# The expert layer's first part: GpSimd's arithmetic moved to VectorE, and one-hots of eight tokens made at once

## The chip, the cores and the metric

One NeuronCore of a Trainium2 chip runs the whole program; the other seven cores are idle. The metric is device time in microseconds (us) of one execution. The kernel before takes 5999.07 us (median of three executions, 5996.86 to 6004.16).

## What is computed

A two-layer backbone of a latent generator: 512 latent and 256 context tokens of width 1024. Layer 0 mixes tokens with an mLSTM, layer 1 with a Mamba-2 scan, and each is followed by a channel mixer out of 16384 single-neuron experts ("PEER"), which is where this change lies:

```python
def block(xb):                                   # 128 tokens
    q = (xb @ wq).reshape(P_BLOCK, P_HEADS, 2, P_DK // 2)
    s = jnp.einsum('thcd,hcnd->thcn', q, sub_keys)
    s_top, i_top = lax.top_k(s, P_TOPK)          # 16 of 128 keys, both halves
    ...
    best_s, best_j = lax.top_k(cand_s, P_TOPK)   # 16 of 256 pairs
    idx = jnp.take_along_axis(cand_i, best_j, axis=-1)
    gate = jax.nn.softmax(best_s, axis=-1)
    act = jax.nn.gelu(jnp.einsum('td,thkd->thk', xb, u[idx]))
    return jnp.einsum('thk,thkd->td', gate * act, v[idx])
```

Each token thus picks 8 heads x 16 experts, an expert being a row of `u` and a row of `v`, and adds up gate x gelu(u.x) x v.

## The kernel before

**Two ways for the experts.** Of the four latent tiles of 128 tokens, three are done densely by `peer_lat` (L895): the scores of *all* 16384 experts are computed, multiplied by a table of gates that is zero where an expert wasn't picked, and multiplied with `v`. The fourth tile, and the context tokens before it, gather their rows with indirect DMAs (`gather_steps`, issued by GpSimd at L864, read by VectorE at L871 and L882).

**The expert layer's first part**, once in each layer, is the stage that the change touches. It has two streams of work that are written interleaved:

- *Score steps* (`prefix`, L907, which calls `scores`, L973). A step covers 128 experts. It loads 512 KB of `u` (`raw`), and `wpair` (L170) splits each half into a rounded part `whi` (ScalarE, L177) and the rest `wlo` (L179, a subtraction of 128x512 elements); 24 products on TensorE (L212 to L214, 128x384) and a gelu (L981) follow, and the result goes to the DRAM tensor `aD`. There are NPRE = 66 such steps. `wlo` is made by VectorE, but for the first UPX = 36 steps by GpSimd: 36 x 2 = 72 subtractions in each layer.
- *Gate steps* (`gate_steps`, L983), which write the gate table `gD`. For each of three tiles `select` (L803) first picks the 16 best of each head on VectorE (L793 to L845, three large operations a head at L832 to L834). Then, four tokens at a time, VectorE compares the expert's two indices with 0..127 (`oh`, L1016, both at once, 128x1024 elements in bfloat16), GpSimd multiplies the first one-hot by a power of two from the gate (`oa`, L1019, 128x512), VectorE the second by the mantissa (`og`, L1021, 128x1024), and 8 products of 128x128 on TensorE (L1026) make the gates of these four tokens, which ScalarE copies out (`sg`, L1028). 32 groups a tile, 96 in a layer, 192 in all.

```python
due = (i2 + 1) * PER          # PER = 2.2
while made < due:
    made += 1
    next(gates_, None)
```

So about two gate steps are written behind each score step, and some gather steps of the fourth tile beside them (`tick`, at rates R_PRA, R_PRE and R_PR1). This is the written order only: a scheduler takes all instructions and puts them in an order of its own on each engine, by its model of when their inputs are ready. An engine then keeps to that order. The dense part behind the stage (`dense`, L1033) needs the gates of all tokens, so it starts when the last gate group is written.

Buffers that matter: `oh` 2, `oa` 2, `og` 2, `sg` 2, the halves `whi` and `wlo` 3 each, two banks `mx` for the gate products.

Of the kernel before, what the change touches and what calls it, by code (L numbers as in the profile page):

```python
# [8 lines left out]
F32 = mybir.dt.float32  # L9
# [36 lines left out]
DTN, SB0, ZD, HV = 1, 0, 1, 1  # L46
PER = 2.2
NPG1, R_PR1 = 46, 1.0
GOP = 1
UP = "v"  # L50
UPX = 36
GS = 10
CSP = 3
SEL = 99
# [15 lines left out]
def backbone(ctx: ExitStack, tc: tile.TileContext, A: dict, out: bass.AP):  # L70
# [732 lines left out]
    def select(pp, vt, it, tag=""):  # L803

        itf = pp.tile([P, PH, 2, TOPK], F32, tag="itf", name="itf", bufs=1)
        nc.vector.tensor_copy(itf.rearrange("p h c k -> p (h c) k"), it)
        nc.vector.tensor_scalar(itf[:, :, 0], itf[:, :, 0], float(PK), None, op0=OP.mult)
        v4 = vt.rearrange("p (h c) k -> p h c k", c=2)
        csb, cib = big_g(pp), big_g(pp)
        cs, ci = [b[:, :PH * NCAND].rearrange("p (h c) -> p h c", h=PH) for b in (csb, cib)]  # L810
        for dst_, a in ((cs, v4), (ci, itf)):
            o = 0
            for r, n in SEGS:
                (nc.gpsimd if CSP & (1 if dst_ is cs else 2) else nc.vector).tensor_tensor(dst_[:, :, o:o + n], a[:, :, 0, r:r + 1].to_broadcast([P, PH, n]),
                                        a[:, :, 1, 0:n], OP.add)
# [12 lines left out]

        pick = csb[:, :NCAND * TOPK].rearrange("p (c k) -> p c k", k=TOPK)
        oh = cib[:, 512:1024].bitcast(BF16)[:, :NCAND * TOPK].rearrange("p (c k) -> p c k", k=TOPK)  # L830
        for hd in range(PH):
            nc.vector.tensor_tensor(oh, placek, bjb[:, hd, None, :].to_broadcast([P, NCAND, TOPK]), OP.is_equal)  # L832
            nc.vector.tensor_tensor(pick, oh, ci[:, hd, :, None].to_broadcast([P, NCAND, TOPK]), OP.mult)  # L833
            nc.vector.tensor_reduce(fi[:, hd], pick.rearrange("p c k -> p k c"), AX.X, OP.add)  # L834
            if hd % SEL == SEL - 1:
                yield
        idx = pp.tile([P, PH * TOPK], I32, tag="idx" + tag, name="idx", bufs=2)
        nc.vector.tensor_copy(idx, fi.rearrange("p h k -> p (h k)"))
        gt = pp.tile([P, PH, TOPK], F32, tag="gt" + tag, name="gt", bufs=2)
# [55 lines left out]
    def peer_lat(i, h, pp, then=lambda: None, close=lambda: None):  # L895


        nt = LAT // P
        nd = NDENSE
        TD = nd * P  # L900
        gD = tc.dram_tile([PK // GJ, P, TD, GJ], F32, name=f"gD{i}")
        aD = tc.dram_tile([NPRE, P, TD], F32, name=f"aD{i}")
        with tc.tile_pool(name="pt", bufs=1, reuse_waits="tile") as xp:
            xh = xp.tile([P, 8, LAT], F32R, name="pinh")
            xl = xp.tile([P, 8, LAT], F32R, name="pinl")

            def prefix(i2):  # L907
                w = xp.tile([P, TD], F32, tag="w", name="w", bufs=3)
                scores(xp, i, i2, xh, xl, TD, w, nc.gpsimd if i2 < UPX or UP[i2 % len(UP)] == "p" else None)
                nc.sync.dma_start(aD[i2], w)  # L910

            back["rate"] = R_WQ
            vt, it = peer_scores(xp, i, 0, LAT, h, xh, xl)
            back["rate"] = 0.0
            before, aside = back["steps"], []

            def rest():
                yield from before
                aside.append(then())
                yield  # L920
                for t in range(nd, nt):
                    yield from gather_steps(pp, i, 0, h(t), h(t), vt[t], it[t])

            back["steps"] = rest()
            with tc.tile_pool(name="pb", bufs=1, reuse_waits="tile") as bp:
                iot4 = bp.tile([P, P, 4], BF16, name="iot4")
                nc.vector.tensor_copy(iot4, iotk[:, :, None].to_broadcast([P, P, 4]))
                gates_ = itertools.chain(*[gate_steps(pp, bp, vt[t], it[t], gD, t, iot4) for t in range(nd)])
                made = 0
                for i2 in range(NPRE):  # L930
                    prefix(i2)
                    due = (i2 + 1) * PER
# [3 lines that stand above are left out]
                    tick((R_PRE if i2 >= NPG else R_PRA) if i == 0 else (R_PR1 if i2 >= NPG1 else 0))  # L936
                for _ in gates_:
                    pass
            with tc.tile_pool(name="pd", bufs=1, reuse_waits="tile") as dp:
                acc = dense(xp, dp, i, gD, aD, nd, xh, xl)  # L940
        close()
        return aside[0], peer_out(i, h, acc, nd)
# [27 lines left out]
                nc.vector.tensor_tensor(y, y, g, OP.mult)  # L970
                nc.vector.tensor_tensor(h(t), y, b, OP.add)

    def scores(xp, i, i2, xh, xl, TD, w, eng):  # L973

        so = smb()[:, :TD]
        for half, (uh, ul) in enumerate(wpair(A[f"uT{i}"][i2].rearrange("h p c -> p h c"), eng=eng)):
            for k in range(4):
                s = slice(k * P, (k + 1) * P)
                kk = half * 4 + k
                mm3(so, uh[:, s], ul[:, s], xh[:, kk, :TD], xl[:, kk, :TD], kk == 0, kk == 7)  # L980
        nc.scalar.activation(w, so, AF.Gelu_apprx_tanh)  # L981

    def gate_steps(pp, bp, vt, it, gD, t, iot4):  # L983
# [13 lines left out]
        nc.tensor.transpose(o[:, 2 * P:3 * P], gt, ident)  # L997

        ct = bp.tile([P, 3, P], BF16, tag="ct", name="ct", bufs=2)
        nc.scalar.copy(ct[:, :2].rearrange("p c t -> p (c t)"), o[:, :2 * P])  # L1000
        gs = bp.tile([P, 2, P], F32, tag="gs", name="gs", bufs=1)
        g_, e_ = gs[:, 0], gs[:, 1]
        nc.scalar.copy(g_, o[:, 2 * P:3 * P])
# [6 lines left out]
        nc.vector.scalar_tensor_tensor(cm[:, 1], g_, 2.0 ** GS, cm[:, 0], OP.mult, OP.subtract)  # L1010
        for q in range(P // GT):
            sg = bp.tile([P, PK // GJ, GT, GJ], F32, tag="sg", name="sg", bufs=2)
            for r in range(GT // 4):
                n = slice(q * GT + r * 4, q * GT + r * 4 + 4)
                oh = bp.tile([P, 2, P, 4], BF16, tag="oh", name="oh", bufs=2)
                nc.vector.tensor_tensor(oh, iot4[:, None].to_broadcast([P, 2, P, 4]),  # L1016
                                        ct[:, 0:2, None, n].to_broadcast([P, 2, P, 4]), OP.is_equal)
                oa = bp.tile([P, P, 4], BF16, tag="oa", name="oa", bufs=2)
                (nc.gpsimd if GOP else nc.vector).tensor_tensor(oa, oh[:, 0], ct[:, 2, None, n].to_broadcast([P, P, 4]), OP.mult)  # L1019
                og = bp.tile([P, 2, P, 4], F16, tag="og", name="og", bufs=2)  # L1020
                nc.vector.tensor_tensor(og, oh[:, 1, None].to_broadcast([P, 2, P, 4]),  # L1021
                                        cm[:, :, None, n].to_broadcast([P, 2, P, 4]), OP.mult)
                g4 = mxb()
                for k in range(4):
                    for u in range(2):
                        nc.tensor.matmul(g4[:, k * P:(k + 1) * P], oa[:, :, k], og[:, u, :, k], start=u == 0, stop=u == 1)  # L1026
                yield
                nc.scalar.activation(sg[:, :, r * 4:r * 4 + 4], g4.rearrange("p (t g j) -> p g t j", t=4, j=GJ),  # L1028
                                     AF.Copy, scale=2.0 ** -GS)
            c0 = t * P + q * GT  # L1030
            nc.sync.dma_start(gD[:, :, c0:c0 + GT].rearrange("g p t j -> p g t j"), sg)

    def dense(xp, dp, i, gD, aD, nd, xh, xl):  # L1033
# [4 lines left out]
        def weights(i2):  # L1038
# [554 lines left out]
```

## Time and profile before

| | us |
|---|---|
| median of the three executions | 5999.07 |
| the profiled execution, on the device | 6006.95 |
| its span, first to last instruction | 6004.9 |
| TensorE busy (products) | 5313.7 (88%) |
| VectorE busy | 4773.5 (79%) |
| GpSimd busy | 2319.6 (39%) |
| ScalarE busy | 2265.9 (38%) |

The stage lies at about 2376 to 2941 us (layer 0) and 4640 to 5166 us (layer 1), counted from the first comparison of the key scores (L793) to the last gate group. In the page, PE is TensorE's products, PEld its weight loads, DVE VectorE, ACT ScalarE, POOL GpSimd and SP the queue of plain DMAs. Shares of busy time are averages over stages with different limits, so the stage is looked at by itself. The granted clock of TensorE is 0.935 over the span.

### The profile page before, as it was taken

How to read it: one execution, taken by the hardware profiler on the slowest of the kernel's cores; microseconds unless marked ns; L12 is line 12 of the kernel's file. 1: busy time of each engine (PE TensorE's matmuls, PEld its weight loads, DVE VectorE, ACT ScalarE, POOL GpSimd, SP SyncE). 2: the span in 40 equal slices, each digit the busy share in tenths (PEclk: the TensorE clock that was granted, in tenths of full speed). 3: DMA queues.
4: the chain of work that ended last, by engine and by line, in shares of the span. 5: the costliest groups of instructions: out<-in, count | busy, mean ns of one | idle time of the engine just before them, and what ended most of it. 6: DMA issues, size and time to landing. Idle time of an engine off the chain costs nothing. (4 is left out here: it accounts for less than half of the span.)

```text
span 6004.9 us, 77193 instructions
## 1 busy us (share of the span) xinstructions
PE 5313.7 (88%) x25708; PEld 4364.4 (73%) x25708; DVE 4773.5 (79%) x8768; ACT 2265.9 (38%) x4218; POOL 2319.6 (39%) x1908
## 2 busy tenths in 40 slices
PE   6899899999997876888799999789877989799998
PEld 4678777766663454788678999667656879678997
DVE  6744567777676788999888889777886999788988
ACT  4543454322222332334333333443323334333333
POOL 1300001355544345474333445433441475433443
PEclk8999999999998897989899999899978989899999
DMA  6755454898879987456698999333334347799996
GB/s 210 239 185 157 159 169 157 294 338 302 305 251 325 331 292 244 142 171 214 227 324 320 341 340 330 131 94 108 95 105 127 108 142 243 269 339 325 345 340 235
DMA packets 655801, 1406.98 MB, mean 234 GB/s; under 512 B 62761, under 2 KB 237497, under 8 KB 650921
## 3 DMA queue, kind: packets, MB, share of 16 engines
q1 hardware_dynamic: 507944, 865.11, 43.6%
q0 software_dynamic: 147456, 536.94, 25.4%
q8 instruction: 202, 3.31, 0.2%
q14 instruction: 199, 1.62, 0.1%
HBM read 1278.10 MB, written 123.70 MB: 233 GB/s over the span
## 5 line engine op out<-in xcount | busy, mean ns | idle before, releaser
L177 ACT CAST whi<-raw 128x512 fp32r<-128x512 f32 x2032 | 1227.2, 619 | 1810.1 <-PE mm L213 614.5
L179 DVE TENSOR_TENSOR wlo<-raw,whi 128x512 fp32r<-128x512 f32 x1787 | 1240.4, 710 | 437.7 <-ACT whi L177 419.6
L864 POOL DMA_INDIRECT g<-in_u_dram,idx x512 | 654.6, 1279 | 1055.0 <-PE mx L214 324.2
L864 POOL DMA_INDIRECT g<-in_v_dram,idv x512 | 685.5, 1339 | 686.0 <-DVE acc L882 293.5
L882 DVE SCALAR_TENSOR_TENSOR acc<-g,act,acc 128x1024 f32<-128x1024 f32 x508 | 664.4, 1308 | 149.0 <-DMA g<-in_v_dram,idv 145.8
L871 DVE CUSTOM_DVE_ANT_0 g<-g,xb 128x1024 f32<-128x1024 f32 x512 | 627.6, 1230 | 185.8 <-DMA g<-in_u_dram,idx 181.4
L214 PE MATMUL sm<-pinh,wlo 128*128 128x384 f32 x2048 | 708.5, 347 | 19.2 <-POOL wlo L179 11.7
L212 PE MATMUL sm<-pinh,whi 128*128 128x384 f32 x2048 | 710.4, 347 | 15.8 <-ACT w L981 13.3
L213 PE MATMUL sm<-pinl,whi 128*128 128x384 f32 x2048 | 707.1, 345 | 0.0
L179 POOL TENSOR_TENSOR wlo<-raw,whi 128x512 fp32r<-128x512 f32 x245 | 365.3, 1501 | 430.5 <-ACT whi L177 403.6
L213 PE MATMUL mm<-wlo,wh 128*128 128x512 f32 x1024 | 399.6, 393 | 17.1 <-DVE wlo L179 17.1
L214 PEld LDWEIGHTS sm<-pinh,wlo 128*128 128x128 f32 x2048 | 395.3, 193 | 26.1 <-POOL wlo L179 15.5
L212 PEld LDWEIGHTS sm<-pinh,whi 128*128 128x128 f32 x2048 | 396.2, 193 | 23.8 <-ACT w L981 14.9
L213 PEld LDWEIGHTS sm<-pinl,whi 128*128 128x128 f32 x2048 | 396.1, 193 | 5.5
L214 PE MATMUL mm<-whi,wl 128*128 128x512 f32 x1024 | 394.7, 392 | 1.6 <-DVE wl L190 1.6
L212 PE MATMUL mm<-whi,wh 128*128 128x512 f32 x1024 | 362.2, 395 | 35.3 <-ACT wh L189 33.1
L1019 POOL TENSOR_TENSOR oa<-oh,ct 128x512 bf16<-128x512 bf16 x192 | 283.2, 1488 | 249.0 <-PE mx L1026 117.9
L213 PE MATMUL mm<-xcl,whi 128*128 128x256 f32 (+1 forms) x1024 | 349.7, 346 | 6.6 <-DVE xcl L190 6.6
L212 PE MATMUL mm<-xch,whi 128*128 128x256 f32 (+1 forms) x1024 | 344.8, 349 | 6.3 <-ACT xch L189 4.0
L214 PE MATMUL mm<-xch,wlo 128*128 128x256 f32 (+1 forms) x1024 | 332.4, 350 | 19.4 <-DVE wlo L179 19.1
L212 PE MATMUL mm<-inh,whi 128*128 128x512 f32 (+1 forms) x768 | 283.8, 373 | 10.4 <-ACT cva L405 4.7
L213 PE MATMUL mm<-inl,whi 128*128 128x512 f32 (+1 forms) x768 | 278.4, 364 | 0.0
(478 smaller groups left out, 11493.7 us busy)
## 6 DMA issues: line engine op xcount, KB each, us to landing
raw<-in_uT_dram SPq DMA_DIRECT2D x256, 512.0 KB
raw<-in_v_dram SPq DMA_DIRECT2D x256, 512.0 KB
raw<-in_w_qk_dram SPq DMA_DIRECT2D x128, 512.0 KB
raw<-in_ada_w_dram SPq DMA_DIRECT2D x96, 512.0 KB
raw<-in_w_up_dram SPq DMA_DIRECT2D x96, 512.0 KB
gD<-sg SPq DMA_DIRECT2D x48, 1024.0 KB
gtb<-gD SPq DMA_DIRECT2D x32, 1536.0 KB
raw<-in_s_in_dram SPq DMA_DIRECT2D x72, 512.0 KB
```

The lines of the kernel that those rows point to most:

```text
L177: nc.scalar.copy(hi, raw[:, u])
L179: (eng or next(los["eng"])).tensor_tensor(lo, raw[:, u], hi.bitcast(F32), OP.subtract)
L212: nc.tensor.matmul(o, sh, mh, start=start, stop=False)
L213: nc.tensor.matmul(o, sh, ml, start=False, stop=False)
L214: last["pe"] = nc.tensor.matmul(o, sl, mh, start=False, stop=stop)
L864: d = nc.gpsimd.indirect_dma_start(out=g_, out_offset=None, in_=tab, in_offset=bass.IndirectOffsetOnAxis(ap=ix[:, k:k + 1], axis=0))
L871: nc.vector.tensor_tensor_reduce(out=g_, in0=g_, in1=xb, scale=1.0, scalar=0.0, op0=OP.mult, op1=OP.add, accum_out=act[:, k:k + 1])
L882: nc.vector.scalar_tensor_tensor(acc, g_, act[:, k:k + 1], acc, OP.mult, OP.add)
L1019: (nc.gpsimd if GOP else nc.vector).tensor_tensor(oa, oh[:, 0], ct[:, 2, None, n].to_broadcast([P, P, 4]), OP.mult)
```

## The change

Four things change, all in this stage:

1. `scores` no longer hands an engine to `wpair`: the `wlo` of all 66 steps is VectorE's (144 subtractions move from GpSimd).
2. The groups are now pairs of groups: `oh` of eight tokens is one comparison of 128x2048, and `oa` of eight tokens is one product of 128x1024, on VectorE instead of GpSimd. `og` and the products on TensorE stay as they are, four tokens at a time.
3. For this the two index columns are laid out alternately in blocks of four tokens (`c2`), by two copies on ScalarE where there was one.
4. `oh` has one buffer instead of two (of twice the size), and `idx` and `gt` of the dense tiles one instead of two.

```diff
-GOP = 1
-UP = "v"
-UPX = 36
...
-        idx = pp.tile([P, PH * TOPK], I32, tag="idx" + tag, name="idx", bufs=2)
+        idx = pp.tile([P, PH * TOPK], I32, tag="idx" + tag, name="idx", bufs=2 if tag else 1)
...
-                scores(xp, i, i2, xh, xl, TD, w, nc.gpsimd if i2 < UPX or UP[i2 % len(UP)] == "p" else None)
+                scores(xp, i, i2, xh, xl, TD, w)
...
-        nc.scalar.copy(ct[:, :2].rearrange("p c t -> p (c t)"), o[:, :2 * P])
+        c2 = ct[:, :2].rearrange("p c t -> p (c t)").rearrange("p (g c t) -> p g c t", c=2, t=4)
+        for c in range(2):
+            nc.scalar.copy(c2[:, :, c], o[:, c * P:(c + 1) * P].rearrange("p (g t) -> p g t", t=4))
...
-            for r in range(GT // 4):
-                n = slice(q * GT + r * 4, q * GT + r * 4 + 4)
-                oh = bp.tile([P, 2, P, 4], BF16, tag="oh", name="oh", bufs=2)
-                nc.vector.tensor_tensor(oh, iot4[:, None].to_broadcast([P, 2, P, 4]),
-                                        ct[:, 0:2, None, n].to_broadcast([P, 2, P, 4]), OP.is_equal)
-                oa = bp.tile([P, P, 4], BF16, tag="oa", name="oa", bufs=2)
-                (nc.gpsimd if GOP else nc.vector).tensor_tensor(oa, oh[:, 0], ct[:, 2, None, n].to_broadcast([P, P, 4]), OP.mult)
...
+            for r in range(GT // 8):
+                n0 = q * GT + r * 8
+                oh = bp.tile([P, 4, P, 4], BF16, tag="oh", name="oh", bufs=1)
+                nc.vector.tensor_tensor(oh, iot4[:, None].to_broadcast([P, 4, P, 4]),
+                                        c2[:, n0 // 4:n0 // 4 + 2].rearrange("p g c t -> p (g c) t")[:, :, None].to_broadcast([P, 4, P, 4]),
+                                        OP.is_equal)
+                ohc = oh.rearrange("p (g c) k t -> p g c k t", c=2)
+                oa = bp.tile([P, 2, P, 4], BF16, tag="oa", name="oa", bufs=2)
+                nc.vector.tensor_tensor(oa, ohc[:, :, 0],
+                                        ct[:, 2, n0:n0 + 8].rearrange("p (g t) -> p g t", t=4)[:, :, None].to_broadcast([P, 2, P, 4]),
+                                        OP.mult)
+                for f in range(2):
+                    n = slice(n0 + f * 4, n0 + f * 4 + 4)
+                    og = bp.tile([P, 2, P, 4], F16, tag="og", name="og", bufs=2)
+                    nc.vector.tensor_tensor(og, ohc[:, f, 1, None].to_broadcast([P, 2, P, 4]),
+                                            cm[:, :, None, n].to_broadcast([P, 2, P, 4]), OP.mult)
```

**The order on VectorE, first stage, around the first gate groups.** `g` and `fi` are the picking of the best experts, `bs`, `smx` and `gt` belong to it too. Before:

```order
L1016 TENSOR_TENSOR oh<-iot_19888,ct 128x1024
L834 TENSOR_REDUCE fi<-g 128x16
L832 TENSOR_TENSOR g<-placek,bjb 128x800
L845 TENSOR_TENSOR gt<-gt,smx 128x128
L1021 TENSOR_TENSOR og<-oh,cm 128x1024 x2
L833 TENSOR_TENSOR g<-g 128x800
```

With the change (line numbers are those of the changed kernel, where L176 is the subtraction that makes `wlo`, L829 to L831 the picking, L1017 `oh`, L1022 `oa` and L1028 `og`):

```order
L1028 TENSOR_TENSOR og<-oh,cm 128x1024 x2
L176 TENSOR_TENSOR wlo<-raw,whi 128x512
L830 TENSOR_TENSOR g<-g 128x800
L176 TENSOR_TENSOR wlo<-raw,whi 128x512
L1017 TENSOR_TENSOR oh<-iot_19888,ct 128x2048
L176 TENSOR_TENSOR wlo<-raw,whi 128x512
L831 TENSOR_REDUCE fi<-g 128x16
L829 TENSOR_TENSOR g<-placek,bjb 128x800
L1022 TENSOR_TENSOR oa<-oh,ct 128x1024
L1028 TENSOR_TENSOR og<-oh,cm 128x1024 x2
```

The subtractions for the scores now stand in VectorE's queue between the picking and the gate groups. The score steps have moved forward: on TensorE the first gate product stands behind 15.6 score steps before and 25.6 now (second layer: 17.6 and 24.6).

**The order on VectorE, end of the second stage.** `g,act` is the dot product with a gathered row (L871, now L868). Before:

```order
L1016 TENSOR_TENSOR oh<-iot_39715,ct 128x1024 x2
L179 TENSOR_TENSOR wlo<-raw,whi 128x512
L871 ISA g,act<-g,xb 128x1024
L871 ISA act 128x1
L179 TENSOR_TENSOR wlo<-raw,whi 128x512
L1021 TENSOR_TENSOR og<-oh,cm 128x1024 x2
```

With the change:

```order
L1028 TENSOR_TENSOR og<-oh,cm 128x1024 x2
L868 ISA g,act<-g,xb 128x1024
L868 ISA act 128x1
L1017 TENSOR_TENSOR oh<-iot_39526,ct 128x2048
L1022 TENSOR_TENSOR oa<-oh,ct 128x1024
L1028 TENSOR_TENSOR og<-oh,cm 128x1024 x2
L1017 TENSOR_TENSOR oh<-iot_39526,ct 128x2048
```

The scores are over by then, and gate groups stand alone: behind the 66th score step 46 of the 96 groups are left in the second layer (14 before) and 32 in the first (7 before).

**The order on GpSimd, first stage.** Before:

```order
L1019 TENSOR_TENSOR oa<-oh,ct 128x512 x2
L179 TENSOR_TENSOR wlo<-raw,whi 128x512 x3
L1019 TENSOR_TENSOR oa<-oh,ct 128x512 x2
L179 TENSOR_TENSOR wlo<-raw,whi 128x512 x2
L864 DMA g<-in_v_dram,idv 128x1024
L179 TENSOR_TENSOR wlo<-raw,whi 128x512
```

With the change, where L811 and L814 are the sums of candidate pairs and L861 is the issue of a gather:

```order
L814 TENSOR_TENSOR g<-itf 128x8x8
L861 DMA g<-in_v_dram,idv 128x1024 x5
L811 TENSOR_TENSOR g<-ptv 128x8x16
L811 TENSOR_TENSOR g<-ptv 128x8x8
L811 TENSOR_TENSOR g<-ptv 128x8x5
```

The 72 subtractions and 96 products of each layer are gone from GpSimd; what is left there stands in the same order as before.

## Rows read from the trace of the kernel before

**Rows 1.** Busy by stretch: from:to, length, PE, PEld, DVE, ACT, POOL us, then clock.
```profile
2376.00:2941.00 565.00, 484.11 (x2798) 447.89 (x2796) 543.13 (x1252) 207.04 (x366) 303.76 (x273) 0.91 0.57 179
4640.00:5166.00 526.00, 470.98 (x2746) 439.89 (x2744) 497.29 (x1211) 198.76 (x355) 291.48 (x259) 0.93 0.55 169
...
2559.00:2722.00 163.00, 139.73 (x804) 132.25 (x803) 158.43 (x231) 61.56 (x111) 111.78 (x96) 0.90 0.55 173
2722.00:2823.00 101.00, 101.00 (x656) 97.95 (x654) 93.42 (x114) 45.51 (x83) 50.40 (x36) 1.00 0.74 229
4950.00:5060.00 110.00, 110.00 (x716) 106.82 (x715) 96.49 (x123) 49.52 (x93) 55.32 (x40) 1.00 0.71 219
```

**Rows 2.** Groups of instructions, whole span: count, busy us, mean ns, idle before.
```profile
L1021 DVE TENSOR_TENSOR og<-oh,cm 128x1024 f16<-128x1024 bf16 x192 | 204.9, 1085 | 23.1 <-PE mx L1026 21.1 <-PE sm L214 1.9
L1016 DVE TENSOR_TENSOR oh<-iot,ct 128x1024 bf16<-128x1024 bf16 x192 | 163.2, 863 | 4.2 <-ACT ct L1000 2.4 <-POOL oa L1019 1.6
...
L834 DVE TENSOR_REDUCE fi<-g 128x16 f32<-128x800 f32 x80 | 123.3, 1541 | 0.6
...
L833 DVE TENSOR_TENSOR g<-g 128x800 f32<-128x800 bf16 x80 | 98.5, 1231 | 0.6
L832 DVE TENSOR_TENSOR g<-placek,bjb 128x800 bf16<-128x800 bf16 x80 | 68.4, 855 | 0.1
...
L806 DVE CAST itf<-pti 128x256 f32<-128x256 uint16 x10 | 13.6, 1364 | 0.0
...
L845 DVE TENSOR_TENSOR gt<-gt,smx 128x128 f32<-128x128 f32 x10 | 10.7, 1068 | 0.0
```

**Rows 3.** The same view of VectorE, first and second stage alone.
```profile
L179 DVE TENSOR_TENSOR wlo<-raw,whi 128x512 fp32r<-128x512 f32 x85 | 62.4, 735 | 1.2 <-ACT whi L177 1.2
...
L179 DVE TENSOR_TENSOR wlo<-raw,whi 128x512 fp32r<-128x512 f32 x84 | 65.0, 780 | 3.6 <-ACT whi L177 3.6
...
L871 DVE CUSTOM_DVE_ANT_0 g<-g,xb 128x1024 f32<-128x1024 f32 x19 | 27.9, 1467 | 3.0 <-DMA g<-in_u_dram,idx 3.0
```

**Rows 4.** The same view of VectorE, 1020 to 1100 us, where GpSimd does little arithmetic.
```profile
L834 DVE TENSOR_REDUCE fi<-g 128x16 f32<-128x800 f32 x8 | 12.3, 1533 | 0.2
...
L833 DVE TENSOR_TENSOR g<-g 128x800 f32<-128x800 bf16 x8 | 7.9, 993 | 0.2
L871 DVE CUSTOM_DVE_ANT_0 g<-g,xb 128x1024 f32<-128x1024 f32 x4 | 4.8, 1222 | 3.9 <-DMA g<-in_u_dram,idx 3.9
L832 DVE TENSOR_TENSOR g<-placek,bjb 128x800 bf16<-128x800 bf16 x8 | 4.6, 571 | 0.0
...
L806 DVE CAST itf<-pti 128x256 f32<-128x256 uint16 x2 | 0.6, 279 | 0.0
...
L845 DVE TENSOR_TENSOR gt<-gt,smx 128x128 f32<-128x128 f32 x1 | 0.3, 296 | 0.0
```

**Rows 5.** Timeline of the second stage, one round of VectorE, then GpSimd.
```profile
4984.59 0.69 DVE L1021 TENSOR_TENSOR og<-oh,cm 128x1024 f16<-128x1024 bf16 x1 [0.74 <-PE mx L1026]
4985.53 1.19 DVE L1021 TENSOR_TENSOR og<-oh,cm 128x1024 f16<-128x1024 bf16 x1 [0.25 <-PE mx L1026]
4986.65 1.53 DVE L1016 TENSOR_TENSOR oh<-iot,ct 128x1024 bf16<-128x1024 bf16 x1
4988.10 0.68 DVE L179 TENSOR_TENSOR wlo<-raw,whi 128x512 fp32r<-128x512 f32 x1
4988.70 0.68 DVE L1016 TENSOR_TENSOR oh<-iot,ct 128x1024 bf16<-128x1024 bf16 x1
4989.30 0.68 DVE L179 TENSOR_TENSOR wlo<-raw,whi 128x512 fp32r<-128x512 f32 x1
...
4984.63 3.00 POOL L1019 TENSOR_TENSOR oa<-oh,ct 128x512 bf16<-128x512 bf16 x2 [3.14 <-PE mx L1026]
```

**Rows 6.** The page, GpSimd's two costliest arithmetic groups.
```profile
L179 POOL TENSOR_TENSOR wlo<-raw,whi 128x512 fp32r<-128x512 f32 x245 | 365.3, 1501 | 430.5 <-ACT whi L177 403.6
...
L1019 POOL TENSOR_TENSOR oa<-oh,ct 128x512 bf16<-128x512 bf16 x192 | 283.2, 1488 | 249.0 <-PE mx L1026 117.9
```

More of the change, by code (lines that the diff above doesn't have):

```diff
@@ L836, in select @@
                 yield
-        idx = pp.tile([P, PH * TOPK], I32, tag="idx" + tag, name="idx", bufs=2)
+        idx = pp.tile([P, PH * TOPK], I32, tag="idx" + tag, name="idx", bufs=2 if tag else 1)
         nc.vector.tensor_copy(idx, fi.rearrange("p h k -> p (h k)"))
-        gt = pp.tile([P, PH, TOPK], F32, tag="gt" + tag, name="gt", bufs=2)
+        gt = pp.tile([P, PH, TOPK], F32, tag="gt" + tag, name="gt", bufs=2 if tag else 1)
         nc.vector.tensor_tensor(gt, bs, bs[:, :, 0:1].to_broadcast([P, PH, TOPK]), OP.subtract)
@@ L971, in peer_out, with scores @@
                 nc.vector.tensor_tensor(h(t), y, b, OP.add)
-    def scores(xp, i, i2, xh, xl, TD, w, eng):
+    def scores(xp, i, i2, xh, xl, TD, w):
         so = smb()[:, :TD]
-        for half, (uh, ul) in enumerate(wpair(A[f"uT{i}"][i2].rearrange("h p c -> p h c"), eng=eng)):
+        for half, (uh, ul) in enumerate(wpair(A[f"uT{i}"][i2].rearrange("h p c -> p h c"))):
             for k in range(4):
@@ L1012, in gate_steps @@
             sg = bp.tile([P, PK // GJ, GT, GJ], F32, tag="sg", name="sg", bufs=2)
-            for r in range(GT // 4):
-                n = slice(q * GT + r * 4, q * GT + r * 4 + 4)
-                oh = bp.tile([P, 2, P, 4], BF16, tag="oh", name="oh", bufs=2)
-                nc.vector.tensor_tensor(oh, iot4[:, None].to_broadcast([P, 2, P, 4]),
-                                        ct[:, 0:2, None, n].to_broadcast([P, 2, P, 4]), OP.is_equal)
-                oa = bp.tile([P, P, 4], BF16, tag="oa", name="oa", bufs=2)
-                (nc.gpsimd if GOP else nc.vector).tensor_tensor(oa, oh[:, 0], ct[:, 2, None, n].to_broadcast([P, P, 4]), OP.mult)
[L1020 to L1029, printed above, removed]
@@ new lines, in gate_steps @@
+            for r in range(GT // 8):
[14 more added lines that the diff above has]
+                                            cm[:, :, None, n].to_broadcast([P, 2, P, 4]), OP.mult)
+                    g4 = mxb()
+                    for k in range(4):
+                        for u in range(2):
+                            nc.tensor.matmul(g4[:, k * P:(k + 1) * P], oa[:, f, :, k], og[:, u, :, k],
+                                             start=u == 0, stop=u == 1)
+                    yield
+                    r4 = r * 8 + f * 4
+                    nc.scalar.activation(sg[:, :, r4:r4 + 4], g4.rearrange("p (t g j) -> p g t j", t=4, j=GJ),
+                                         AF.Copy, scale=2.0 ** -GS)
@@ L1047, in weights @@
             else:
-                scores(xp, i, i2, xh, xl, TD, w, None)
+                scores(xp, i, i2, xh, xl, TD, w)
             nc.vector.tensor_tensor(w, w, gt[0][:, :, j], OP.mult)
```

## Prediction

> **What bounds the kernel now.** The change touches one stage in each layer, so I read the busy time by stretch first, then the groups of VectorE's instructions, then a timeline.
>
> In the two stages VectorE is busy for 543.1 of 565 us and 497.3 of 526 us; TensorE for 484.1 and 471.0, ScalarE for some 200 each [rows 1]. So VectorE is the bound over the whole, with 22 and 29 us idle, and TensorE is next, with 81 and 55 us to spare. It isn't so in every stretch: where experts are being picked (2559 to 2722 us) VectorE is busy 158.4 of 163 us while TensorE has gaps and is granted 0.90 of its clock, a mean between its two levels of 1.2 and 2.4 GHz; in the middle of each stage (101 and 110 us) TensorE is full at clock 1.00, and VectorE has 7.6 and 13.5 us idle [rows 1].
>
> The second thing to see is that VectorE's time isn't all its own. The comparison `oh` takes 0.68 us in the timeline where nothing runs on GpSimd, and 1.53 us when GpSimd works on `oa`; `og` takes 0.69 and 1.19 [rows 5]. Over the whole run `oh` has a mean of 863 ns and `og` of 1085 [rows 2]. The large operations of the picking are the same: 1231 and 855 ns (L833, L832) [rows 2], against 993 and 571 in a stretch where GpSimd hardly computes [rows 4]. So the time that GpSimd "saves" is partly paid back by VectorE. One round of the timeline prices it: GpSimd's two `oa` take 3.00 us, and cost VectorE 0.50 + 0.85 = 1.35 us [rows 5].
>
> **The change, part by part.** All in VectorE's time, in both layers together.
>
> *Added: 144 subtractions* (`wlo`). One follows the next at 0.60 us (4988.10 to 4988.70) [rows 5]: +86.4 us.
>
> *Added: 96 products `oa` of 1024 elements.* VectorE has made none yet. The nearest row is `oh`, also 1024 bfloat16 elements from two bfloat16 inputs with one broadcast: 0.60 us from its start to the next (4988.70 to 4989.30) [rows 5]. +57.6 us. The ends: 0.49 us, which is the 571 ns of 800 elements [rows 4] less the same overlap of 0.08, and 1.20 us, if it goes at the pace of `wlo`, 512 elements in 0.60 us [rows 5]. I take 0.60, since type and form are those of `oh`.
>
> *Changed: 192 comparisons of 1024 become 96 of 2048.* From 800 to 1024 elements is 571 to 680 ns, 0.49 ns an element [rows 4, 5]; so 2048 take 0.68 + 0.50 = 1.18 us, less the overlap of 0.08, 1.10. Two small ones take 1.20. That is 96 x 0.10 = 9.6 us gained: doing eight tokens at once is a small thing by itself. The upper end is 2.40 us, at the pace of `wlo`.
>
> *Removed: what GpSimd costs VectorE.* Mean less undisturbed duration, by count [rows 2 to 5]: `og` (1085 - 690) x 192 = 75.8; `oh` (863 - 680) x 192 = 35.1; L833 (1231 - 993) x 80 = 19.0; L832 (855 - 571) x 80 = 22.7; L806 (1364 - 279) x 10 = 10.9; L845 (1068 - 296) x 10 = 7.7; `wlo` (735 - 680) x 85 + (780 - 680) x 84 = 13.1; L871 (1467 - 1222) x 19 = 4.7. Together 189 us. Smaller groups would add to this. The upper end goes by GpSimd's own time: 283.2 us of `oa` and 144 x 1.50 = 216 us of `wlo` [rows 6], 499 us, at 1.35 for each 3.00 [rows 5], is 225 us. The lower end leaves out what lies where TensorE is full: 101 + 110 us [rows 1] in rounds of 3.00 + 3.14 us [rows 5] are 34 rounds of 1.35 us, 46 us; 143 us remain. I take 189, because the order brings the score steps forward (25.6 of them ahead of the first gate product instead of 15.6), out of these full stretches and into the picking, where TensorE has gaps; behind the last score step 46 and 32 gate groups then stand alone, where VectorE alone sets the pace: a pair of groups takes 1.10 + 0.60 + 2 x 0.60 = 2.90 us there.
>
> How the reduction reads: L834 has 1541 ns over the run and 1533 undisturbed [rows 2, 4], so it is hardly slowed, while operations with two tensor inputs are. The Trainium skill ("SBUF — State Buffer", section "Who interferes with whom") states this: a VectorE instruction with two SBUF inputs contends with a GpSimd instruction that reads SBUF, `tensor_reduce` never does, and the second to issue fully blocks. By its full block the return would be anything up to the whole 499 us, depending on who came first; the measured 1.35 in 3.00 decides, and the sum stays with 189.
>
> *Edits at nothing.* The second copy of the index columns on ScalarE, six times in all, is one small operation ahead of the first `oh` of a tile: I put 1 us for it. `oh` with one buffer: its readers `oa` and `og` are now all on VectorE ahead of the next `oh`, so order alone protects it; if `oa` were still elsewhere, each pair would wait for it. `idx` and `gt` with one buffer: their readers come right behind the picking, a tile ahead of the next writer. GpSimd's queue loses 72 + 96 instructions a layer, and the gathers that stood behind them can go earlier; VectorE reads those where its order says, so this gives nothing; its waits for them are 3.0 us in the second stage [rows 3]. On the queue of plain DMAs the loads of `raw` come earlier with their steps; no wait on them stands in VectorE's rows [rows 3].
>
> *The new wait.* `wlo` now stands behind `og` in VectorE's queue, and `og` waits for TensorE to free its buffer: 0.74 + 0.25 us a round [rows 5], 21.1 us in all [rows 2]. TensorE's next scores wait for that `wlo`. I leave this idle time as it is.
>
> *Sum.* 86.4 + 57.6 - 9.6 - 189 + 1 = -54 us (rounded), with VectorE as the bound and its idle time unchanged. Against the profiled execution of 6006.95 us that is 5953; the median shown is 7.9 us lower, and against it the forecast is 5999 - 54 = **5945 us**. What is late next is TensorE: its spare 81 and 55 us are more than the 27 or so that each stage would lose.
>
> **Rivals.**
>
> *More comes back* (up to the 225 us): -54 - 36 = -90, 5909 us. For it: many small operations of the picking, not in my sum, share the port as well. Against it: VectorE and TensorE come nearer to each other, and some of the gain is lost in waits.
>
> *TensorE keeps the middle.* If the full stretches stay, only 143 us return: -8, 5991 us, no difference. For it: the two full stretches are there now [rows 1]. Against it: the order.
>
> *Head-of-line waits, the other side.* GpSimd's `wlo` fed TensorE whatever VectorE was waiting for; now one queue serves both streams. If each of the 96 pairs waits the 0.99 us of the round shown [rows 5], that is 95 us in place of 21: -54 + 74 = +20, 6019 us. It decides from 54 / 96 = 0.56 us more idle time a pair. Against it: the round shown is from a stretch with TensorE full, and the picking fills VectorE elsewhere.
>
> *The pace is lost.* If the new shapes go at one element a step as `wlo` does, `oa` costs 58 us and `oh` 125 us more: +129, 6128 us. Against it: `oh` has the same broadcast form today, with half the elements.
>
> *A full engine only gets fuller.* If what I read as GpSimd's share didn't come back, the added work stands alone: +134 + 1, 6134 us. Against it: each long `oh` and `og` of the timeline lies on an `oa`. The Trainium skill ("Perfetto Trace Analysis", section "Optimizing Scalar/DVE Operations") has the rule for this side: when VectorE is saturated, handing work to ScalarE or even GpSimd may make sense, though between VectorE and GpSimd it might not help because they share a read port. The trace agrees with the second half of it.
>
> That the change doesn't do what it says can be left out: the order shows `oa` and `wlo` of this stage on VectorE and gone from GpSimd.
>
> **How the numbers follow.** Forecast 0.66, more back 0.15, TensorE keeps the middle 0.10, head-of-line 0.05, pace lost 0.02, full engine 0.02. About 0.2% (12 us) is what a measurement of this kernel can tell from no change: the first two cases are faster (0.81), the third the same (0.10), the others slower (0.09). The range takes in the first three, from 5908 (the upper end of what returns) to 5993 (just past the third).
>
> **What would show it.** Right: `oh` of 2048 near 1.2 us and `oa` near 0.7 in duration, with hardly any spread; `og` near 0.69 and L832, L833 near 571 and 993 throughout; both stages shorter by 20 to 40 us, everything else as before. Wrong: `og` or `wlo` with much more idle time ahead of them (head-of-line), stretches with TensorE full and VectorE idle as long as now (TensorE keeps the middle), or `og` as long as before.

## The result, and the profile after

The changed kernel takes 5940.4 us (median of four runs, 5933.15 to 5946.78) against 6001.6 (four runs, 5996.86 to 6010.03) for the kernel before on the same chip: a ratio of 0.9898 [0.9885, 0.9911], or 61 us less, 53 to 69. The forecast was 54 us less. The profiled execution took 5942.98 us, with a span of 5941.2.

Busy time by stretch, after the change, in the columns of [rows 1]: the two stages from the first comparison of key scores to the last gate group, then the ends of both stages, where gate groups stand alone.

```profile
2373.00:2919.00 546.00, 467.58 (x2787) 434.51 (x2785) 505.40 (x1333) 207.91 (x367) 84.28 (x107) 0.90 0.60 187
4598.00:5098.00 500.00, 458.82 (x2769) 429.28 (x2768) 465.59 (x1311) 202.68 (x360) 53.95 (x91) 0.92 0.56 179
2857.00:2919.00 62.00, 31.24 (x244) 26.73 (x242) 56.37 (x77) 18.36 (x32) 4.07 (x3) 0.50 0.48 147
5020.00:5097.00 77.00, 45.62 (x355) 39.49 (x355) 70.94 (x97) 26.92 (x48) 0.00 (x0) 0.50 0.53 166
```

With the same two marks, the kernel before has

```profile
2378.00:2941.00 563.00, 482.11 (x2785) 446.09 (x2784) 542.02 (x1251) 206.07 (x364) 302.91 (x272) 0.91 0.57 179
4636.00:5166.00 530.00, 474.98 (x2767) 443.29 (x2765) 501.29 (x1237) 199.53 (x357) 291.48 (x259) 0.93 0.54 168
```

The stages lost 17 and 30 us. VectorE, which took over the work of 336 operations of GpSimd in 240 of its own, is busy 36.6 and 35.7 us *less* in them, 72 together; its idle time rose by 19.6 and 5.7 us (21.0 to 40.6, 28.7 to 34.4). The other 17 us of the 64 between the two spans lie outside: 5 ahead of the first stage, 10 in the dense part of layer 0 (841 to 831 us), 6 in the scan between the stages, against 4 lost in the dense part of layer 1. So much can be spread from run to run: in the six runs below whose edits lie in the stages alone (the two halves, both halves by fours, and the three with GpSimd work that nobody waits for), the first stage begins between 2360 and 2378 us, and all that lies outside the stages takes 4879 to 4907 us, against 4912 before and 4895 after.

VectorE's groups over the whole span show why it is busy less. L1028, L1017 and L1022 are `og`, `oh` and `oa`; L831, L830 and L829 are what L834, L833 and L832 were; L803 and L842 what L806 and L845 were.

```profile
L1028 DVE TENSOR_TENSOR og<-oh,cm 128x1024 f16<-128x1024 bf16 x192 | 124.2, 684 | 1.1 <-PE mx L1033 1.0
L831 DVE TENSOR_REDUCE fi<-g 128x16 f32<-128x800 f32 x80 | 123.4, 1542 | 0.3
L1017 DVE TENSOR_TENSOR oh<-iot,ct 128x2048 bf16<-128x2048 bf16 x96 | 117.1, 1220 | 5.1 <-ACT ct L1000 4.1
L830 DVE TENSOR_TENSOR g<-g 128x800 f32<-128x800 bf16 x80 | 78.9, 986 | 0.2
L1022 DVE TENSOR_TENSOR oa<-oh,ct 128x1024 bf16<-128x1024 bf16 x96 | 65.9, 686 | 1.1
L829 DVE TENSOR_TENSOR g<-placek,bjb 128x800 bf16<-128x800 bf16 x80 | 45.4, 567 | 0.1
L803 DVE CAST itf<-pti 128x256 f32<-128x256 uint16 x10 | 3.0, 302 | 0.8 <-POOL g L814 0.7
L842 DVE TENSOR_TENSOR gt<-gt,smx 128x128 f32<-128x128 f32 x10 | 2.8, 282 | 0.0
```

Against [rows 2]: `og` 684 ns for 1085, the two picking products 986 for 1231 and 567 for 855, the cast 302 for 1364. These are the undisturbed durations of [rows 4, 5]. The reduction, which had not been slowed, did not move (1542 for 1541). And `og` waits 1.1 us for its buffer where it waited 23.1.

What VectorE waits for now, longest sums of each stage (line, what it waited for: us in total, times, longest):

```profile
DVE acc L879 <- DMA g<-in_v_dram,idv: 23.2, 13, 4.4
DVE wlo L176 <- ACT whi L174: 5.2, 7, 1.4
...
DVE wlo L176 <- ACT whi L174: 26.4, 21, 2.6
DVE oh L1017 <- ACT ct L1000: 2.7, 1, 2.7
```

In the first stage these are rows of the gathered tile (the sum `acc` of layer 0's context tokens; 3.7 us before the change), in the second ScalarE's `whi` (3.6 before), which itself waits most for TensorE's products to free its buffers. For TensorE now runs nearly full in the middle of each stage for longer, 169 and 233 us where it was 101 and 110 [rows 1], with VectorE idle for 21 and 19 us of these:

```profile
2581.00:2750.00 169.00, 161.05 (x989) 155.90 (x990) 147.66 (x263) 71.97 (x130) 37.36 (x41) 0.98 0.66 210
4787.00:5020.00 233.00, 228.84 (x1432) 222.25 (x1430) 214.42 (x386) 106.55 (x191) 36.00 (x37) 1.00 0.70 231
```

### The profile page after: what moved, and what is told of

Same layout as the page of the kernel before. It is cut to its first block, busy times and chain, and to the rows that moved or that the text cites. A ratio compares the mean times of both kernels' runs of the same rounds, so it can differ in the third digit from the quotient of the medians.

```text
span 5941.2 us, 76363 instructions
## 1 busy us (share of the span) xinstructions
PE 5280.6 (89%) x25708; PEld 4337.6 (73%) x25708; DVE 4692.1 (79%) x8912; ACT 2270.6 (38%) x4224; POOL 1828.1 (31%) x1572
## 3 DMA queue, kind: packets, MB, share of 16 engines
q0 software_dynamic: 147456, 536.94, 25.6%
## 5 line engine op out<-in xcount | busy, mean ns | idle before, releaser
L176 DVE TENSOR_TENSOR wlo<-raw,whi 128x512 fp32r<-128x512 f32 x1931 | 1322.9, 699 | 478.6 <-ACT whi L174 461.4
L861 POOL DMA_INDIRECT g<-in_u_dram,idx x512 | 640.5, 1251 | 1449.7 <-PE mx L211 419.3
L861 POOL DMA_INDIRECT g<-in_v_dram,idv x512 | 685.0, 1338 | 881.3 <-DVE acc L879 320.7
L868 DVE CUSTOM_DVE_ANT_0 g<-g,xb 128x1024 f32<-128x1024 f32 x512 | 622.2, 1219 | 156.9 <-DMA g<-in_u_dram,idx 155.3
L211 PE MATMUL sm<-pinh,wlo 128*128 128x384 f32 x2048 | 692.3, 342 | 14.5 <-DVE wlo L176 14.2
L209 PE MATMUL sm<-pinh,whi 128*128 128x384 f32 x2048 | 695.9, 340 | 3.3 <-ACT w L978 3.2
L210 PE MATMUL sm<-pinl,whi 128*128 128x384 f32 x2048 | 693.5, 339 | 0.0
L1058 DVE TENSOR_TENSOR w<-w,gtb 128x384 f32<-128x384 f32 x256 | 233.5, 915 | 66.7 <-ACT w L978 31.7
L1033 PE MATMUL mx<-og,oa 128*128 128x128 f16 x1536 | 199.1, 297 | 91.7 <-DVE og L1028 91.6
```

Of the source, the lines that this page charges most:

```text
L176: (eng or next(los["eng"])).tensor_tensor(lo, raw[:, u], hi.bitcast(F32), OP.subtract)
L209: nc.tensor.matmul(o, sh, mh, start=start, stop=False)
L210: nc.tensor.matmul(o, sh, ml, start=False, stop=False)
L211: last["pe"] = nc.tensor.matmul(o, sl, mh, start=False, stop=stop)
L861: d = nc.gpsimd.indirect_dma_start(out=g_, out_offset=None, in_=tab, in_offset=bass.IndirectOffsetOnAxis(ap=ix[:, k:k + 1], axis=0))
L868: nc.vector.tensor_tensor_reduce(out=g_, in0=g_, in1=xb, scale=1.0, scalar=0.0, op0=OP.mult, op1=OP.add, accum_out=act[:, k:k + 1])
```

## Experiments

All runs alternate with the kernel before on the same chip; "ratio" is to that, with its 95% interval.

### One half of the move at a time

The kernel before, with only the subtractions on VectorE:

```diff
-UPX = 36
+UPX = 0
```

> The kernel before, with only the 144 subtractions of the scores (wlo) moved to VectorE; oa stays on GpSimd, four tokens at a time. Port theory (GpSimd's arithmetic beside VectorE holds VectorE up): VectorE gets 86 us more and loses the share of wlo, 216 of 499 us of GpSimd's time, 82 to 97 us of the 189 to 225; so within 15 us of before, 5985 to 6015. Order theory (the gain comes from the score steps that move forward, which the order of this kernel shows as well: 25.1 steps ahead of the first gate product): most of the 61 us, 5940 to 5960. Full-engine rival: 86 us slower, 6085.

Measured: 5971.3 us, ratio 0.9954 [0.9937, 0.9971], 29 us less (17 to 38), between the two ranges that were expected.

The kernel before, with only the products `oa` on VectorE:

```diff
-GOP = 1
+GOP = 0
```

> The kernel before, with only oa moved to VectorE (192 products of 512 elements, about 0.35 us each from start to start); wlo of the first 36 steps stays on GpSimd. Its order keeps the score steps where they were (16.1 ahead of the first gate product). Port theory: +67 us on VectorE, and 107 to 128 us of interference gone; 40 to 60 us faster, 5940 to 5960. Order theory: nothing moves forward and VectorE has more to do, 6000 or more. Full-engine rival: 6067.

Measured: 5956.7 us, ratio 0.9927 [0.9909, 0.9944], 44 us less (34 to 55). `oh` and `og` in the two runs, the subtractions' run first:

```profile
L1021 DVE TENSOR_TENSOR og<-oh,cm 128x1024 f16<-128x1024 bf16 x192 | 187.8, 1005 | 0.8 <-issue 0.6
L1016 DVE TENSOR_TENSOR oh<-iot,ct 128x1024 bf16<-128x1024 bf16 x192 | 137.3, 739 | 8.9 <-POOL oa L1019 7.6 <-issue 1.3
```

```profile
L1021 DVE TENSOR_TENSOR og<-oh,cm 128x1024 f16<-128x1024 bf16 x192 | 148.1, 774 | 0.1
L1016 DVE TENSOR_TENSOR oh<-iot,ct 128x1024 bf16<-128x1024 bf16 x192 | 138.7, 741 | 1.8 <-ACT ct L1000 1.8
```

With the subtractions alone moved, `og` still has the 1005 ns of an operation that runs beside GpSimd's `oa`; with `oa` alone moved, 774. So `oa` was `og`'s main disturber; of what `oh` lost, each half gives back about as much (739 and 741 ns, from 863). The second run lies in the range of the port theory and far from the 6000 or more of the order theory. The subtractions gained more than their own balance: VectorE's busy time in the stages fell by 12 us only (542 and 501 to 531 and 500), but the stages by 10 and 13, since `og`'s 21.1 us of waits for TensorE [rows 2] are gone. I put this down to the moved score steps, without a run that moves them alone: ahead of the first gate group TensorE had done 25 of them, as after the change. That the two runs together gain 73 us, more than both edits in one kernel (next), is within their intervals.

### Both halves, without the operations of eight tokens

```diff
-GOP = 1
+GOP = 0
...
-UPX = 36
+UPX = 0
```

> Both moves, but four tokens at a time as before: the change without its operations of eight tokens. Port theory: as the change, plus 10 us for 192 instead of 96 comparisons and 9 us for 192 instead of 96 products: 5950 to 5965. If the operations of eight tokens were what pays: near 6000.

Measured: 5942.8 us, ratio 0.9918 [0.9895, 0.9940], where the whole change has 0.9898 [0.9885, 0.9911]; the profiled spans are 5942.1 and 5941.2. The intervals overlap, so what eight tokens at once bring isn't told from nothing; without them at least 5950 us was expected. Its timeline, where groups stand alone at the end of the first stage, and below it that of the whole change there (start us, us, operation):

```profile
2891.75 1.28 DVE L1016 TENSOR_TENSOR oh<-iot,ct 128x1024 bf16<-128x1024 bf16 x2
2892.95 0.41 DVE L1019 TENSOR_TENSOR oa<-oh,ct 128x512 bf16<-128x512 bf16 x1
2893.29 0.68 DVE L1021 TENSOR_TENSOR og<-oh,cm 128x1024 f16<-128x1024 bf16 x1
2893.89 0.42 DVE L1019 TENSOR_TENSOR oa<-oh,ct 128x512 bf16<-128x512 bf16 x1
2894.22 0.68 DVE L1021 TENSOR_TENSOR og<-oh,cm 128x1024 f16<-128x1024 bf16 x1
2894.83 1.28 DVE L1016 TENSOR_TENSOR oh<-iot,ct 128x1024 bf16<-128x1024 bf16 x2
```

```profile
2888.48 1.22 DVE L1017 TENSOR_TENSOR oh<-iot,ct 128x2048 bf16<-128x2048 bf16 x1
2889.74 0.69 DVE L1022 TENSOR_TENSOR oa<-oh,ct 128x1024 bf16<-128x1024 bf16 x1
2890.35 1.28 DVE L1028 TENSOR_TENSOR og<-oh,cm 128x1024 f16<-128x1024 bf16 x2
2891.67 1.22 DVE L1017 TENSOR_TENSOR oh<-iot,ct 128x2048 bf16<-128x2048 bf16 x1
```

Eight tokens take 3.08 us with operations of four and 3.19 with operations of eight. An operation normally starts 0.07 to 0.08 us before the one ahead of it has ended; `oa` behind the very `oh` that it reads, and `oh` behind the `og` that reads its one buffer, start 0.04 us *after* the end. Two such places cost 0.24 us a pair and eat what fewer instructions save.

### GpSimd work that nobody waits for

The change, with two GpSimd products behind each `oa`, as large as the old `oa`, into a scratch tile that nobody reads:

```diff
+                for _ in range(2):
+                    scr = bp.tile([P, P, 4], BF16, tag="scr", name="scr", bufs=1)
+                    x_ = nc.gpsimd.tensor_tensor(scr, iot4, iot4, OP.mult)
+                    tc.add_manual_dep(x_.ins, d_.ins.name, mybir.DependencyInfo(
+                        mybir.DependencyClass.Sync, mybir.DependencyReason.DATA), reason="beside the one-hots")
```

> The changed kernel with two products of 128x512 bfloat16 on GpSimd behind each oa (192 in all, as many as GpSimd made before), on constants, into a scratch tile that nobody reads. Nothing waits for them. Port theory: 192 x 1.49 us x 0.45 is up to 127 us more on VectorE, less what its idle time (some 70 us in both stages) takes up: 30 to 110 us slower than the change, 5970 to 6050, with og and oh spread out again. Order theory, or any theory by waits for data: as the change, 5940.

Measured: 6035.5 us, ratio 1.0062 [1.0045, 1.0079]: 95 us more than the change. Then the same with fills in place of the products, and with copies:

```diff
-                    x_ = nc.gpsimd.tensor_tensor(scr, iot4, iot4, OP.mult)
+                    x_ = nc.gpsimd.memset(scr, 0.0)
```

> The change, with two GpSimd operations behind every scaled one-hot as in the run with idle products (192 in all), but fills of the same scratch tile with zeros: they read nothing from SBUF and write 128x512 numbers, and nobody waits for them. A theory by which VectorE loses time to GpSimd operations that read SBUF: as the change, 5935 to 5950 us, with oh(2048) at 1.22, og at 0.69 and w lo at 0.68 us. A theory by which any GpSimd operation on SBUF costs VectorE time: slower in proportion to the length of the fills, with the same operations stretched (in the run with products oh(2048) took 1.48 and og 0.93 us).

```diff
-                    x_ = nc.gpsimd.tensor_tensor(scr, iot4, iot4, OP.mult)
+                    x_ = nc.gpsimd.tensor_copy(scr, iot4)
```

> As the run with idle fills, but GpSimd copies a 128x512 table of one input into the scratch tile. If what counts is that GpSimd reads at all, VectorE's operations are stretched while a copy runs as by a product, and the time lies between the change and the products' 6035 in proportion to the copies' length (an estimate: half the reads of a product, so 5965 to 6010). If it takes two inputs on GpSimd to hold VectorE up, as the change, 5935 to 5950.

Measured: fills 5938.9 us, ratio 0.9892 [0.9872, 0.9912], as the change; copies 5974.3 us, ratio 0.9949 [0.9931, 0.9968]. For products, fills and copies in turn, GpSimd's group and VectorE's `oh` and `og`:

```profile
L1027 POOL TENSOR_TENSOR scr<-iot 128x512 bf16<-128x512 bf16 x192 | 293.0, 1526 | 350.4 <-DVE oa L1022 342.8
L1017 DVE TENSOR_TENSOR oh<-iot,ct 128x2048 bf16<-128x2048 bf16 x96 | 141.9, 1478 | 4.0 <-ACT ct L1000 3.0
L1033 DVE TENSOR_TENSOR og<-oh,cm 128x1024 f16<-128x1024 bf16 x192 | 170.5, 926 | 0.1
```

```profile
L1027 POOL MEMSET scr<- 128x512 bf16 x192 | 101.0, 526 | 417.6 <-DVE oa L1022 412.2
L1017 DVE TENSOR_TENSOR oh<-iot,ct 128x2048 bf16<-128x2048 bf16 x96 | 117.2, 1221 | 6.0 <-ACT ct L1000 5.0
L1033 DVE TENSOR_TENSOR og<-oh,cm 128x1024 f16<-128x1024 bf16 x192 | 124.3, 685 | 1.4 <-PE mx L1038 1.3
```

```profile
L1027 POOL COPY scr<-iot 128x512 bf16<-128x512 bf16 x192 | 206.0, 1073 | 363.5 <-DVE oa L1022 357.2
L1017 DVE TENSOR_TENSOR oh<-iot,ct 128x2048 bf16<-128x2048 bf16 x96 | 126.2, 1315 | 4.8 <-ACT ct L1000 3.8
L1033 DVE TENSOR_TENSOR og<-oh,cm 128x1024 f16<-128x1024 bf16 x192 | 146.9, 801 | 2.0 <-PE mx L1038 1.9
```

This settles the mechanism. No engine waits for any of these, so what they cost is interference alone. (Gathers stand behind them in GpSimd's queue; they do so in all three runs, and with fills that costs nothing.) VectorE's busy time in the stages rose by 118 us for 293 us of products (0.40 for each), by 48 for 206 us of copies (0.23), and not at all for 101 us of fills (969 against 971). What GpSimd *reads* costs VectorE here; what it only writes doesn't. The Trainium skill ("SBUF — State Buffer", section "Who interferes with whom") says that an operation of VectorE with two SBUF inputs contends with one of GpSimd that reads SBUF and not with one that only writes it; these three runs agree. They don't show a full block, which the page spells out for VectorE's 2-port modes and the prediction took for these products as well: in 293 us of products VectorE lost 118.

### Is VectorE the bound in the stages?

The change, with no gather steps in the stages, and more of them in the dense part behind:

```diff
-NPG1, R_PR1 = 46, 1.0
+NPG1, R_PR1 = 66, 1.0
-R_PRA = 0.3
+R_PRA = 0.0
-R_UP, R_ATT, R_DN, R_WQ, R_PRE, R_D1, R_D2, R_MOD = 1.7, 6.05, 0.46, 0.5, 0.36, 1.0, 3.47, 1.1
+R_UP, R_ATT, R_DN, R_WQ, R_PRE, R_D1, R_D2, R_MOD = 1.7, 6.05, 0.46, 0.5, 0.0, 1.34, 3.47, 1.1
```

> The change, with no gather steps in the two stages; they are taken up in the dense part that follows, 1.34 for each of its first 66 steps where there was 1. If VectorE's work sets the length of the stages, stage 1 loses the 44.6 us of accumulations and their 23.2 us of waits for gathers, stage 2 its 23.0 us of dots: stages of about 480 and 477 us. The dense part has VectorE busy 241 of 283 us and DMA at 0.92 (stage 1's first 283 us of it): if it has room for the steps, 5855 to 5890 in all; if DMA sets it, it gives back about what the stages gain, 5930 to 5960. If TensorE sets the length of the stages (busy 468 of 546 and 459 of 500), less than 15 us in each, 5910 to 5945.

Measured: 5958.6 us, ratio 0.9924 [0.9908, 0.9941], 18 us more than the change. The stages, then the dense part of layer 0:

```profile
2364.00:2859.00 495.00, 461.21 (x2767) 430.64 (x2765) 439.49 (x1191) 200.00 (x357) 32.78 (x68) 0.94 0.57 178
4612.00:5100.00 488.00, 457.84 (x2767) 428.94 (x2765) 446.30 (x1271) 202.30 (x360) 29.80 (x72) 0.94 0.52 162
2859.00:3763.00 904.00, 806.77 (x3808) 700.59 (x3808) 782.83 (x1161) 321.39 (x583) 368.13 (x294) 0.95 0.89 317
```

VectorE lost 66 and 19 us of work, and the stages 51 and 12 us of length: over the whole VectorE's work sets it. But TensorE is close behind (461 of 495), and the dense part of layer 0 took 904 us in place of 831, that of layer 1 830 in place of 817. In layer 0 the last gathered row was added 57 us behind the last dense product (3759 against 3702 us; 6 us behind it in the change), so the steps that were moved there set its end. The gathers were in a good place.

### Elsewhere, moving GpSimd's arithmetic gains nothing

The change, with the 180 candidate sums on VectorE too, and the change with 53 of the last 101 subtractions too, those in the first 350 us (the edit leaves 48 on GpSimd at 3721 to 3886 us, so it doesn't move the 101 that the expectation speaks of):

```diff
-CSP = 3
+CSP = 0
```

> The change, with the candidate sums (180 small additions, 77 us of GpSimd's time in the whole kernel, about half of it in the stages) on VectorE as well. VectorE takes an estimated 0.15 to 0.28 us each (from 0.21 us for its 128x128 scaling beside them), 27 to 50 us, and gets back 0.23 to 0.40 us for each of the 77, as in the runs with idle copies and products, 18 to 31. In the two stages, where its work sets the length, that is half: between 6 us less and 16 us more, so 5934 to 5956. A theory by which VectorE gains whatever leaves GpSimd: 5925 or less.

```diff
-LO_U = "vvp"
+LO_U = "v"
```

> The change, with the last GpSimd w lo as well (101, 150 us of GpSimd's time) on VectorE; nearly all lie in the first part of the kernel, where VectorE is busy 231 of 350 us and TensorE 288. VectorE takes 101 times 0.68, 69 us, and gets back at most 0.40 of 150, 60. If the gain of the change came from VectorE being the bound in the stages, there is none here: 5935 to 5955. If taking arithmetic from GpSimd gains anywhere, as it did for w lo in the stages (29 us for 144): 5910 to 5925.

Measured: with the sums 5974.8 us, ratio 0.9947 [0.9931, 0.9963], 34 us *more* than the change (29 by the two ratios) and outside what was expected; with the subtractions 5936.0 us, ratio 0.9883 [0.9865, 0.9901], the same. The sums on VectorE:

```profile
L811 DVE TENSOR_TENSOR g<-ptv 128x16 f32<-128x16 f32 (+5 forms) x80 | 11.1, 223 | 0.0
L811 DVE TENSOR_TENSOR g<-itf 128x128 f32<-128x128 f32 (+3 forms) x80 | 10.9, 234 | 0.0
```

Some 27 us of work came to VectorE (with 20 more sums like these) and nothing came back. I argue, without a run for it, that the sums had run beside the search for the 16 best, whose operations showed no stretching beside GpSimd. The two stages, where 144 of the 180 sums lie, grew by 12 and 4 us only; the rest of the 33 us between the spans lies outside them, 7 of it ahead of the first, where runs differ by more without any edit. So what the sums themselves cost is less sure than the 34. The subtractions tell less than I expected: in the first 350 us VectorE is busy 231 to 232, with or without them, since the convolution's operations get back what the subtractions take (L404 went from 689 to 474 ns). VectorE is idle for a third of that stretch and the time stays; but as its busy time stayed too, the run can't tell what it would be worth to shorten it.

### What could be had beyond the change

The change with 74 score steps ahead, to use TensorE's idle end of each stage:

```diff
-NPRE = 66
+NPRE = 74
-R_UP, R_ATT, R_DN, R_WQ, R_PRE, R_D1, R_D2, R_MOD = 1.7, 6.05, 0.46, 0.5, 0.36, 1.0, 3.47, 1.1
+R_UP, R_ATT, R_DN, R_WQ, R_PRE, R_D1, R_D2, R_MOD = 1.7, 6.05, 0.46, 0.5, 0.36, 1.0, 3.83, 1.1
```

> The change, with 74 score steps taken ahead into each stage instead of 66, and 3.83 gather steps for each of the 54 later dense steps where there were 3.47 for each of 62. A dense step that finds its scores takes 4.55 us and one that makes them 8.6 us, so each dense part loses 8 times 4.05, 32 us. In the stages each added step has 16 TensorE products of 0.33 us, 5.3 us, and two w lo of 0.68 us on VectorE. If VectorE's work sets the stages, 11 us more in each: 5895 to 5905. If the added steps run at TensorE's pace and take 8 to 12 of the groups left over (1.9 us each) with them, 19 to 27 us more in each: 5915 to 5930. If the dense part is held by its gathers instead, no gain: 5940 or more.

Measured: 5946.8 us, ratio 0.9900 [0.9880, 0.9921], no gain. The stages grew by 12 and 22 us; the dense part of layer 1 lost 26 and that of layer 0 nothing. (An added step is 24 products, not the 16 of the expectation, and added 4.1 to 4.6 us to TensorE's busy time.) Then a fifth buffer for gathered rows, alone and with the 74 steps:

```diff
-GB = 4
+GB = 5
```

> The change, with five buffers for gathered rows instead of four, so a gather can be asked for one step earlier. After the change VectorE waits 23.2 us for gathers in stage 1, and some 30 us for them in each dense part. If these waits are for the latency of a transfer that is asked for too late, they shrink and stage 1 is 10 to 20 us shorter: 5915 to 5930 in all. If they come from the DMA engines' load or from the pacing by TensorE's products, nothing moves: 5935 to 5950.

> Five buffers for gathered rows (5886 us alone) and 74 score steps ahead with 3.83 gather steps for each later dense step (5947 alone). Alone the steps ahead lengthened the stages by 12 and 22 us and shortened the dense part by 26 us in layer 1 and not at all in layer 0, whose last gather came 12 us ahead of its last product. If the gathers held that dense part, five buffers free it and it loses 20 to 30 us: 5855 to 5875. If the two do not bear on each other, as the sum of the two: 5886 to 5900.

Measured: five buffers 5886.4 us, ratio 0.9794 [0.9778, 0.9810]; both 5869.7 us, ratio **0.9772 [0.9758, 0.9787]**, the fastest of all, 134 us under the kernel before and 71 under the change. The first lies outside both ranges that were expected, and I had the place of the gain wrong. Stage 1 went from 546 to 540 us only; it is the stretch from 1000 us to the first stage that went from 1373 to 1312. VectorE's waits for gathers there, after the change, then with five buffers:

```profile
DVE g L868 <- DMA g<-in_u_dram,idx: 107.6, 80, 5.1
DVE acc L879 <- DMA g<-in_v_dram,idv: 105.6, 88, 5.4
```

```profile
DVE g L868 <- DMA g<-in_u_dram,idx: 41.5, 41, 4.1
DVE acc L879 <- DMA g<-in_v_dram,idv: 28.5, 32, 5.2
```

They fell from 213 to 70 us, 143 less, of which 61 show in the time; VectorE's waits for ScalarE's `whi` there rose from 32.1 to 89.1 us. The dense part of layer 1 is 15 us longer with five buffers (832 for 817), for which I have no shown cause. With five buffers the 74 steps do pay: the dense parts take 806 and 797 us, against 833 and 832 with five buffers alone, and the stages 17 and 25 more. So in layer 0 the gathers had held the dense part: with the 74 steps alone the last gathered row was added 32 us behind the last dense product (3758 against 3726 us; the expectation has it 12 us ahead, which the trace doesn't bear out), and with five buffers 7 us behind it. Five buffers weren't tried in the kernel before; so whether they gain as much without the change is open.

## Why the prediction was right

**The bound.** VectorE over the whole of the stages, as read from [rows 1]; the run without gather steps shows it.

**What came back.** The forecast put the added work at 86.4 + 57.6 - 9.6 = 134.4 us, and VectorE's busy time in the stages fell by 72.3, so 207 us returned, or up to 217 if the 9.6 weren't gained (below): 189 forecast, between the ends of 143 and 225. The row sum was the right way to price it; it left out small groups, as it said, and so came out low. `og` gave 192 x (1085 - 684) = 77.0 us (75.8 forecast). `og` at 684 and the picking at 567 and 986 ns came within 7 ns of what was named beforehand.

**The added operations.** `oa` of eight tokens 0.61 us from its start to the next (0.60 forecast). `wlo` 682 to 684 ns where it was undisturbed (680).

**Operations of eight tokens: mis-sized.** "Two small ones take 1.20", and 9.6 us gained, left out that what reads a result right behind it starts late. A pair takes 3.19 us where groups stand alone, not the 2.90 of the working and not less than the 3.08 of the kernel by fours. "Order alone protects it" of `oh`'s one buffer was true, and not free.

**"I leave this idle time as it is": wrong in both directions.** The wait that the head-of-line rival rested on vanished (23.1 to 1.1 us), as I argue because the score steps had moved forward. Others took its place: gathers in the first stage (23.2 us), ScalarE's `whi` in the second (26.4), and behind that TensorE. Idle time rose by 25 us in all, so the stages lost 47 us, not 54, the first of them 17 where at least 20 were named as a sign of being right; 17 us outside the stages, which the working didn't have and which may be spread from run to run, made up for it. That the total came within 7 us is thus partly luck.

**The rivals.** A full engine that only gets fuller would have been 6134 us; the idle products show why it wasn't. TensorE keeps the middle had its sign: the stretches with TensorE nearly full didn't go, they grew from 211 to 402 us. But 207 us returned all the same, where its price rested on 143. More comes back was near: 207 to 217 lies between 189 and 225, and the new waits ate the difference.

## What to carry to other kernels

When a saturated VectorE hands work to GpSimd, price what VectorE's own operations lose beside it: the mean of each group over the run less its duration in a stretch where GpSimd is quiet, times its count. Here 499 us of GpSimd's subtractions and products cost VectorE some 207 us, more than the 134 or so that it took to do them itself. The same move brought nothing in a stretch where VectorE is idle for a third of the time, and a loss with the small sums, I think because they ran beside operations that GpSimd didn't slow.

When one bound falls, look at the new waits by what they wait for: the waits for gathered rows were in the profile before and after alike, and one more buffer was worth nearly as much as the whole change.

## What the runs showed that I had not expected

- A GpSimd copy of one input costs VectorE too: 0.23 us for each of its own, between the fills' nothing and the products' 0.40.
- An operation that follows the one it depends on starts 0.04 us after its end; an independent one 0.07 to 0.08 us before it.
- At the ends of the stages, where TensorE is busy 31 of 62 and 46 of 77 us, its granted clock is 0.50, the lower of its two levels (1.2 GHz). In the first stage it had 0.98 from 2581 to 2750 us, where TensorE was busy 161 of 169, and 0.83 from 2760 to 2857, where it was busy 73 of 97. I take it that this cost little, since VectorE was busy 56 and 71 us of these ends; no run shows it.
- The cast of one input on VectorE (L806, 128x256) went from a mean of 1364 to 302 ns, though it has no second input. Most of that is two of the ten casts, of 3.83 and 5.83 us, and these were held in full: the first began beside three of GpSimd's subtractions in a row, and ended 0.16 us after the last of them (start us, us, operation):

```profile
2496.41 3.76 POOL L179 TENSOR_TENSOR wlo<-raw,whi 128x512 fp32r<-128x512 f32 x3
2496.50 3.83 DVE L806 CAST itf<-pti 128x256 f32<-128x256 uint16 x1
```

The Trainium skill ("SBUF — State Buffer", section "Who interferes with whom") has casts among the operations that can enter a 2-port mode and then contend with GpSimd; these rows agree. In the run with the products `oa` alone moved, the cast beside three subtractions takes 3.83 us again.
